# Half splits, unit order, early columns, shorter router chains, float32r put-back and an earlier combine in a two-layer backbone kernel

## The chip, the cores and the metric

The kernel runs on one core of a Trainium2 chip. The metric is the device time of one execution in microseconds (us); before the change the median of 3 runs is 1303.72 us (1302.54 to 1303.9). Engines are named as the profile names them: PE (matmul), PEld (its weight load), DVE (vector), ACT (scalar), POOL (GpSimd), SP (only issues DMAs here).

## What is computed

Two layers over 256 context and 256 latent tokens of width 1024, batch 1. Layer 0 mixes tokens with gated DeltaNet heads and S5 groups, layer 1 with latent attention (MLA); each layer ends with a mixture of 16 experts of which a token takes two. The part that the change touches most, cut from the reference:

```python
def grouped_moe(h, router_w, router_bias, w_gate, w_up, w_down):
    tok = h.reshape(-1, h.shape[-1])
    scores = jax.nn.sigmoid((tok @ router_w).astype(F32))
    choice = scores + router_bias.astype(F32)
    ...  # the best group of 4 experts, in it the best two
    wts = wts / jnp.sum(wts, axis=-1, keepdims=True)
    gates = jnp.sum(jax.nn.one_hot(idx, N_EXPERTS, dtype=F32) * wts[..., None], axis=1)
    for e in range(N_EXPERTS):
        act = jax.nn.silu(tok @ w_gate[e]) * (tok @ w_up[e])
        out = out + gates[:, e:e + 1] * (act @ w_down[e])
...
x = x + g1 * o_l
x = x + g2 * grouped_moe(modulate(x, norm2_g[i], sh2, sc2), ...)   # the context tokens too in layer 0
return rmsnorm(x, final_norm_g)
```

In layer 0 the experts see 512 tokens, in layer 1 the 256 latent ones. An expert's weights are 6 MB in float32, all 32 experts' 201 MB.

## The kernel before

**Stages.** Projections of layer 0 with S5, DeltaNet preparation and the adaLN weights (to about 375 us); DeltaNet solve and scan (to 480); output projection and norm (to 538); router 0 (to 556); experts 0 (to 853); put-back (to 884); MLA (to 1015); output projection 1 and norm (to 1060); router 1 (to 1077); experts 1 (to 1295); final norm.

**Order.** Each engine runs its own queue in order. The last lines of `kernel()` build the program with `schedule_with_timeline_sim=True`: the build lays the order of each queue itself, from the order of the code, the data dependencies and its own estimate of times. So two neighbouring lines need not be neighbours in a queue. `tc.issue_after(ins)` keeps what is written in its block behind `ins` on the same engine. In the first stage five generators are interleaved by hand: each digit of `ORDER` (L42) gives one turn to one of S5, its tables, the chain gates - norm of k - decays - inverses, the projections, and the loads of the adaLN weights (L987).

**Expert weights** come in 1 MB chunks of 128 x 2048 float32, by DMAs on SP's queue, into a ring of slots (9 in layer 0); a chunk is loaded when its slot is free. In layer 0 places 0 and 1 are fixed experts, so their chunks are fetched ahead of the router's result; SP has to read the number of any other expert (`m.exi`) first.

**Experts 0** (L1618 to 1817). Tokens are sorted to tiles of 128 rows, 13 of them, gathered from `h2d`. The units of `order` (L1759) are of three kinds: a *pair* of experts that share a tile, 64 rows each, in float32 (12 MB, 12 chunks); *[1, 2]*, two tiles of one expert; and single tiles of one expert. The last two run in float32r, a quicker matmul type, with both operands split in a hi and a lo part: `wsplit` (L1659) makes hi by an ACT copy and lo = w - hi by DVE or POOL, whole chunks, three hi/lo buffers in turn; `mm3` multiplies xh*wh, xh*wl, xl*wh for each block of 128 rows, so 12 matmuls a chunk. The loop over units runs the gate half 0 of the next unit, turns the activations of this one, runs gate half 1, `write` (down projection, scatter of the rows to `yd` by POOL), then the up halves of the next. For the last unit `put_back` (L1684) is used: its rows are put to the tokens by a one-hot matmul, and `combine` (L1676), called between, reads the two rows of every token from `yd` (four 1 MB reads through the same ring), adds them (POOL), scales and adds them to x (DVE). Then loops over overflow tiles, which run no turn here, make every engine wait for the others.

**Layer 1.** `moe_open` (L1280) loads what the router needs, among it `cols` (L1312): the shift and scale of the second norm as columns, two reads of single elements, 8 KB, from the adaLN result `modd`. PE makes the router's constant `cst` from them, DVE the scaled router weights `rws`, which also need the norm gains `gc2`. It is called inside `out_proj1` (L1252) between the two halves of the projection. `moe_norm` (L1339) makes the logits and, in `late`, h2, on POOL for the last tile of a layer. `experts1` (L1836) takes seven tiles, all in float32, picks the tokens by a one-hot matmul, and `put_back` (L1904) multiplies a gated one-hot `sT` with y in float32: four matmuls a tile. In the trace a float32 matmul leaves two records, a float32r matmul one.

Of the kernel before, what the change touches and what calls it, by code (L numbers as in the profile page):

```python
# [10 lines left out]
F32 = mybir.dt.float32  # L11
F32R = mybir.dt.float32r
I32 = mybir.dt.int32
# [28 lines left out]
ORDER = "14043434201412034140300224440414102414430241041040042342334021201104444404001320040143444401421224440444323042414011111344042423434004400004124041144320420442404440404412324332041440133004030404444034224404143244402404441244"  # L42
# [123 lines left out]
def _build(es, tc, I, O):  # L166
# [75 lines left out]

    n1g = per.tile([128, 2, 8], F32, name="n1g")
    nc.scalar.dma_start(n1g.rearrange("p a b -> p (a b)"), I["norm1_g"])
    mcols = per.tile([128, 2, 2, 2, 8], F32, name="mcols")

# [1040 lines left out]
    def moe_open(l, stack):  # L1287
# [53 lines left out]
    def moe_norm(m, i, t):  # L1341
# [29 lines left out]
    def moe_route(m):  # L1371
# [116 lines left out]
        tt(oh, bc(sm[:, SM_IO16:SM_IO16 + 16, None], SQ), bc(pos[:, None, :], SQ), OP.is_equal)  # L1488
        tt(oh, oh, bc(sm[:, None, SM_IO16:SM_IO16 + 16], SQ), OP.mult)
        red(key[:, :, None], oh, OP.add)  # L1490
        m.exi = rt([128, 16], I32, True)
        V.tensor_copy(m.exi, key)

# [18 lines left out]
        for j in range(2 * n):  # L1512
            kk, i = j // n, j % n
            V.tensor_scalar(m.ohS[:, kk, i], m.io[:, 0:128], rin[:, kk, i], None, op0=OP.is_equal)
# [4 lines left out]
        m.rest = lambda: moe_tables(m, rt, tt, red, oa, sc, table, ovs)  # L1519
# [92 lines left out]
    def experts0(m):  # L1612
        with ExitStack() as st:
# [8 lines left out]
            cnt3, gathers, last_split = [0], [], []  # L1622
# [48 lines left out]
            def mm3(p, xh, xl, wh, wl, start, stop):  # L1671
                mm(p, xh, wh, start, False)
                mm(p, xh, wl, False, False)
                mm(p, xl, wh, False, stop)
# [10 lines left out]
            def put_back(ps_, tok, tok2, gate, between=lambda: None):  # L1685
# [11 lines left out]
                between()  # L1697
# [520 lines left out]
```

## Time and profile before

| | |
|---|---|
| median of 3 runs | 1303.72 us |
| the profiled execution | 1306.65 us, its span 1304.8 us |
| PE busy | 1132.8 us (87%), 6208 matmuls, mean granted clock 0.939 |
| DVE, ACT, POOL busy | 687.2, 420.5, 320.6 us |
| DMA | 342.44 MB, mean 262 GB/s |

The span is the time from the first to the last instruction; the profiled execution's own time is 1.85 us longer. Busy shares are means over stages that have different limits, so they are read by stage. The page's chain of the work that ended last stops at the overflow loop of layer 1, 10 us before the end, and so says nothing of the rest. Granted clock 1.00 is PE at 2.4 GHz, 0.50 at 1.2 GHz.

### The profile page before, as it was taken

What the parts mean: (1) busy time and instruction counts of PE and PEld (TensorE: products, weight loads), DVE (VectorE), ACT (ScalarE), POOL (GpSimd) and SP (SyncE); (2) the same over time, 40 slices, a digit from 0 to 9 for tenths busy, and PEclk for the clock granted to TensorE, in tenths of its full rate; (3) what the DMA queues carried; (4) which work ended last, traced back from release to release, by engine and by line L of the source; (5) the groups of instructions that cost most, each with busy time, mean ns of one, the idle gap of its engine ahead of it and who ended that gap; (6) DMA issues with size and microseconds to landing.
All of it is one profiled execution on the core that took longest, in us unless ns stands there. A gap on an engine that the chain in (4) does not pass through costs nothing. (4 is left out here: it accounts for less than half of the span.)

```text
span 1304.8 us, 17075 instructions
## 1 busy us (share of the span) xinstructions
PE 1132.8 (87%) x6208; PEld 711.9 (55%) x6208; DVE 687.2 (53%) x1393; ACT 420.5 (32%) x694; POOL 320.6 (25%) x249
## 2 busy tenths in 40 slices
PE   4698989998769998598998998867999749999996
PEld 1365656665329987434455646645777645444321
DVE  3979796757954574812325536685576251221122
ACT  3324635452112242112336446615455101100000
POOL 0255553311315330310214213333321020000000
PEclk9799999899879999799998999978999869999998
DMA  8565565688886155879999899453134666999993
GB/s 319 200 206 163 201 204 196 213 295 221 273 218 243 58 184 146 347 268 420 369 381 381 329 397 362 175 229 122 48 132 148 230 274 258 425 425 423 426 425 164
DMA packets 110456, 342.44 MB, mean 262 GB/s; under 512 B 35210, under 2 KB 53002, under 8 KB 84000
## 3 DMA queue, kind: packets, MB, share of 16 engines
q1 hardware_dynamic: 81328, 312.02, 63.0%
q10 hardware_dynamic: 24352, 17.93, 4.5%
q0 software_dynamic: 4688, 11.35, 2.4%
q8 instruction: 51, 0.84, 0.3%
q14 instruction: 37, 0.30, 0.1%
HBM read 319.45 MB, written 26.77 MB: 265 GB/s over the span
## 5 line engine op out<-in xcount | busy, mean ns | idle before, releaser
L209 PE MATMUL ps<-hi,sp 128*128 128x512 f32 x432 | 145.5, 411 | 8.0 <-ACT hi L1667 5.3
L1668 DVE TENSOR_TENSOR lo<-ch,hi 128x2048 fp32r<-128x2048 f32 x40 | 98.5, 2474 | 80.3 <-ACT hi L1667 79.9
L209 PE MATMUL ps<-ch,stat 128*32 128x512 f32 x384 | 91.7, 686 | 28.4 <-DMA ch<-in_ada_w 14.4
L209 PE MATMUL ps<-ch,xT 128*64 128x512 f32 (+1 forms) x488 | 106.8, 596 | 0.0
L209 PEld LDWEIGHTS ps<-hi,sp 128*128 128x128 f32 x432 | 83.4, 195 | 35.1 <-ACT hi L1667 8.5
L1667 ACT ACTIVATE hi<-ch 128x2048 fp32r<-128x2048 f32 x48 | 91.7, 1916 | 29.4 <-issue 10.7
L209 PE MATMUL ps<-lo,sp 128*128 128x512 f32 x216 | 88.9, 412 | 12.8 <-POOL lo L1668 10.0
L209 PE MATMUL ps<-ch,wh 128*64 128x512 f32 x384 | 93.4, 598 | 2.2 <-DMA ch<-in_wu 2.2
L209 PE MATMUL ps<-hH,wh 128*128 128x512 f32 x160 | 66.8, 419 | 5.9 <-ACT hH L658 5.6
L209 PE MATMUL ps<-hH,wl 128*128 128x512 f32 x160 | 65.2, 409 | 1.8 <-DVE wl L605 1.8
L209 PE MATMUL ps<-hL,wh 128*128 128x512 f32 x160 | 66.2, 414 | 0.4 <-DVE hL L659 0.2
L209 PEld LDWEIGHTS ps<-ch,xT 128*64 128x64 f32 (+1 forms) x488 | 32.5, 129 | 58.4 <-issue 57.7
L231 POOL TENSOR_TENSOR frs<-rs,sm 128x1 f32<-128x1 f32 x2 | 1.1, 560 | 234.2 <-DVE rs L230 234.2
L209 PEld LDWEIGHTS ps<-lo,sp 128*128 128x128 f32 x216 | 42.1, 195 | 28.1 <-POOL lo L1668 11.9
L209 PEld LDWEIGHTS ps<-ch,wh 128*64 128x64 f32 x384 | 27.5, 136 | 54.8 <-issue 50.7
L1668 POOL TENSOR_TENSOR lo<-ch,hi 128x2048 fp32r<-128x2048 f32 x8 | 36.6, 4574 | 69.3 <-ACT hi L1667 54.0
L209 PE MATMUL ps<-ch,aT 128*64 128x512 f32 (+1 forms) x232 | 51.9, 596 | 0.7 <-ACTq L1579 0.7
L605 POOL TENSOR_TENSOR wl<-raw,wh 128x1024 fp32r<-128x1024 f32 x16 | 40.8, 2553 | 35.8 <-ACT wh L604 23.3
L1902 DVE TENSOR_TENSOR y<-ps,bcm 128x512 f32<-128x512 f32 x14 | 9.7, 692 | 73.8 <-PE ps L209 73.8
L1627 POOL DMA_INDIRECT xe<-h2d,rt x13 | 15.5, 1193 | 132.3 <-PE ps L206 119.7
L209 PEld LDWEIGHTS ps<-ch,stat 128*32 128x32 f32 x384 | 13.6, 116 | 62.6 <-DMA ch<-in_ada_w 30.4
L209 PE MATMUL ps<-y,sT 128*128 128x512 f32 x72 | 37.9, 659 | 9.5 <-DVE y L1695 7.9
(536 smaller groups left out, 2376.8 us busy)
## 6 DMA issues: line engine op xcount, KB each, us to landing
ch<-in_wg SPq DMA_DIRECT2D x63, 1024.0 KB, 6.4
ch<-in_wu SPq DMA_DIRECT2D x62, 1024.0 KB, 11.1
ch<-in_wd SPq DMA_DIRECT2D x61, 1024.0 KB, 10.6
ch<-in_ada_w SPq DMA_DIRECT2D x88, 512.0 KB, 5.6
raw<-in_w_in SPq DMA_DIRECT2D x16, 512.0 KB, 4.9
bcm<-modd ACTq DMA_DIRECT2D x12, 512.0 KB, 16.2
x<-in_xs SPq DMA_DIRECT2D x8, 512.0 KB, 6.0
yd<-x SPq DMA_DIRECT2D x8, 512.0 KB, 4.9
```

The lines of the kernel that those rows point to most:

```text
L209: return T.matmul(out, l, r, start=start, stop=stop)
L231: G.tensor_tensor(out, t, bc(neghalf, [128, n]), op=OP.pow)
L605: eng.tensor_tensor(wl, w, wh.bitcast(F32), op=OP.subtract)
L1627: g = G.indirect_dma_start(out=xe, out_offset=None, in_=h2d, in_offset=bass.IndirectOffsetOnAxis(ap=idx, axis=0), bounds_check=511, oob_is ...
L1667: last_split[:] = (S.activation(hi, w, AF.Copy), eng.tensor_tensor(lo, w, hi.bitcast(F32), op=OP.subtract))
L1668: eng.tensor_tensor(lo, w, hi.bitcast(F32), op=OP.subtract))
L1902: V.tensor_tensor(j.y[:, nh], p, g2[:, nh * 512:(nh + 1) * 512], op=OP.mult)
```

## The change

- `ORDER` becomes another string of the same 224 digits' counts.
- `wsplit` splits in halves: two ACT copies, then two subtractions, the first on DVE, the second on the engine given; that is POOL for gate half 1 and up half 0 (before: POOL for the whole of up half 0), else DVE. `mm3` becomes `mm3q`: all eight matmuls with hi of a chunk, then the four with lo.
- The units: [1, 2] second, the pairs third, seventh and last, so the last unit is a pair. `combine` stands ahead of the last down projection.
- In `moe_route` the experts' numbers `exi` and `moe_tables` move into `rest`, behind the last one-hot of DVE's queue. In `late` the second multiply goes from POOL to ACT.
- `rope` and `mg` are loaded ahead of router 0, the layer-1 columns (`cols1`) after experts 0.
- In experts 1 `sT` is ungated and float32r, y is scaled by gate and g2 in one DVE operation and split in hi and lo, and the put-back is two float32r matmuls for each one before. The tiles sl, act, aT, sT and y have one buffer.

The diff, cut:

```diff
+    cols1 = per.tile([128, 2, 8], F32, name="cols1")
...
-            cols = m.mh.tile([128, 2, 8], F32, name=f"cols{c}")
-            nc.scalar.dma_start(cols, modd[l, c, 3 * D:5 * D].rearrange("(j k p) -> p j k", j=2, p=128))
+            cols = cols1 if l else m.mh.tile([128, 2, 8], F32, name=f"cols{c}")
+            if l == 0:
+                mod_cols(cols, l, c)
...
-                E.tensor_scalar(h2, h2, m.rstd[:, i:i + 1], None, op0=OP.mult)
+                S.activation(h2, h2, AF.Copy, scale=m.rstd[:, i:i + 1])
...
-        m.rest = lambda: moe_tables(m, rt, tt, red, oa, sc, table, ovs)
+        def rest():
+            with tc.issue_after(last.ins):
+                tt(oh, bc(sm[:, SM_IO16:SM_IO16 + 16, None], SQ), bc(pos[:, None, :], SQ), OP.is_equal)
...
+                V.tensor_copy(m.exi, key)
+                moe_tables(m, rt, tt, red, oa, sc, table, ovs)
...
-                last_split[:] = (S.activation(hi, w, AF.Copy),
-                                 eng.tensor_tensor(lo, w, hi.bitcast(F32), op=OP.subtract))
+                halves = [(slice(0, 2), V), (slice(2, 4), eng)]
+                for s, _ in halves:
+                    S.activation(hi[:, s], w[:, s], AF.Copy)
+                for s, e in halves:
+                    e.tensor_tensor(lo[:, s], w[:, s], hi[:, s].bitcast(F32), op=OP.subtract)
...
+            def mm3q(p, xT, k0, w, start, stop):
+                for q in range(4):
+                    for i in range(2):
+                        mm(p, xT[i][:, k0 + q], w[0][:, q], start and q + i == 0, False)
+                for q in range(4):
+                    mm(p, xT[0][:, k0 + q], w[1][:, q], False, stop and q == 3)
...
-                wh, wl = wsplit(gate_up_chunk(0, name, u[0].es[0](), hh), G if (name, hh) == ("wu", 0) else V)
+                w = wsplit(gate_up_chunk(0, name, u[0].es[0](), hh), G if (name, hh) in (("wg", 1), ("wu", 0)) else V)
...
-            order = [([0], [0, 1]), ([10], [10, 11]), ([1, 2], [2]), ([11], [12, 13]), one[3], one[4], one[5],
-                     ([12], [14, 15]), one[6], one[7], one[8], one[9]]
+            order = [([0], [0, 1]), ([1, 2], [2]), ([10], [10, 11]), one[3], one[4], one[5],
+                     ([11], [12, 13]), one[6], one[7], one[8], one[9], ([12], [14, 15])]
...
+            combine()
             p = [p for _, _, p in down(cur)]
-            put_back(p, m.tokf[:, cs], tokm[:, cs], m.gate[:, cs], combine)
+            put_back(p, m.tokf[:, cs], tokm[:, cs], m.gate[:, cs])
...
-                V.tensor_scalar(j.sT, m.io, j.tok, j.gate, op0=OP.is_equal, op1=OP.mult)
+                V.tensor_scalar(j.sT, m.io, j.tok, None, op0=OP.is_equal)
...
-                    V.tensor_tensor(j.y[:, nh], p, g2[:, nh * 512:(nh + 1) * 512], op=OP.mult)
+                    V.scalar_tensor_tensor(y, p, j.gate, g2[:, nh * 512:(nh + 1) * 512], op0=OP.mult, op1=OP.mult)
+                    parts_of(hi, lo, y, V)
...
-                        mm(p, j.sT[:, i * 128:(i + 1) * 128], j.y[:, nh], True, True)
+                        for part, y in enumerate(j.y):
+                            mm(p, j.sT[:, i * 128:(i + 1) * 128], y[:, nh], part == 0, part == 1)
...
+    nc.scalar.dma_start(rope.rearrange("p a b c -> p (a b c)"), I["c_rope"])
+    nc.scalar.dma_start(mg, I["mla_g"])
...
+    mod_cols(cols1, 1, 0)
```

## Rows read from the trace of the kernel before

**Rows 1.** Stages: window, length; PE, PEld, DVE, ACT, POOL busy; clock, DMA share, GB/s.

```profile
538.00:556.00 18.00, 3.01 (x62) 2.56 (x62) 16.36 (x83) 0.26 (x1) 5.91 (x3) 0.50 0.96 403
556.00:853.00 297.00, 273.36 (x1200) 163.51 (x1197) 122.67 (x87) 133.86 (x124) 73.52 (x33) 0.97 0.85 339
853.00:884.20 31.20, 18.51 (x46) 10.01 (x44) 26.28 (x23) 0.60 (x1) 11.25 (x4) 0.78 0.59 229
...
1077.00:1282.00 205.00, 202.53 (x1040) 84.13 (x1042) 36.81 (x70) 18.01 (x29) 0.00 (x0) 0.99 0.96 399
```

**Rows 2.** Waits of PE, 556 to 885: total us, times, longest us.

```profile
PE ps L209 <- POOL lo L1668: 10.0, 4, 3.4
...
PE ps L209 <- ACT hi L1667: 5.3, 4, 1.6
...
PE ps L209 <- DVE lo L1668: 2.7, 4, 1.3
PE ps L209 <- DMA ch<-in_wu: 2.2, 1, 2.2
```

**Rows 3.** In order of time, experts 0: start, us, engine, operation [idle before].

```profile
611.33 2.28 DVE L1668 TENSOR_TENSOR lo<-ch,hi 128x2048 fp32r<-128x2048 f32 x1
628.47 4.54 POOL L1668 TENSOR_TENSOR lo<-ch,hi 128x2048 fp32r<-128x2048 f32 x1
629.66 5.52 DVE L1668 TENSOR_TENSOR lo<-ch,hi 128x2048 fp32r<-128x2048 f32 x1 [16.04 <-ACT hi L1667]
692.12 0.79 PE L209 MATMUL ps<-lo,sp 128*128 128x512 f32 x1 [3.42 <-POOL lo L1668]
```

**Rows 4.** Groups of instructions, whole span: busy us, mean ns of one.

```profile
L1667 ACT ACTIVATE hi<-ch 128x2048 fp32r<-128x2048 f32 x48 | 91.7, 1916 | 29.4 <-issue 10.7
...
L605 POOL TENSOR_TENSOR wl<-raw,wh 128x1024 fp32r<-128x1024 f32 x16 | 40.8, 2553 | 35.8 <-ACT wh L604 23.3
...
L604 ACT ACTIVATE wh<-raw 128x1024 fp32r<-128x1024 f32 x16 | 16.9, 1056 | 35.1 <-PE ps L209 19.1 <-DMA dcd<-x 6.6 <-DMA raw<-in_w_in 5.6
```

**Rows 5.** In order of time: PE at the same place of two single units.

```profile
800.61 0.49 PE L209 MATMUL ps<-hi,sp 128*128 128x512 f32 x1 [1.13 <-ACT hi L1667]
...
820.85 0.50 PE L209 MATMUL ps<-hi,sp 128*128 128x512 f32 x1 [1.13 <-ACT hi L1667]
821.82 0.50 PE L209 MATMUL ps<-hi,sp 128*128 128x512 f32 x1 [0.47 <-ACT sp L1640]
```

**Rows 6.** In order of time: the end of layer 0.

```profile
853.61 2.20 SPq L1680 DMA_DIRECT2D ch<-yd  x4
858.68 11.34 POOL L1681 TENSOR_TENSOR ch<-ch 128x1024 f32<-128x1024 f32 x4 [7.35 <-DMA ch<-yd]
872.35 10.11 PE L209 MATMUL ps<-y,sT 128*128 128x512 f32 x16 [7.90 <-DVE y L1695]
881.67 2.47 DVE L1702 TENSOR_TENSOR x<-x,ps 128x512 f32<-128x512 f32 x4
```

**Rows 7.** In order of time: the output projection of layer 1.

```profile
1039.83 1.22 DVE L1305 SCALAR_TENSOR_TENSOR bcm<-bcm,bcm 128x1024 f32<-128x1024 f32 x1 [4.78 <-DMA bcm<-modd]
1041.94 3.56 PE L209 MATMUL ps<-rw,cols 128*128 128x16 f32 x16 [7.67 <-DMA cols<-modd]
1045.34 7.02 PE L209 MATMUL ps<-ch,oT 128*128 128x512 f32 x22
1054.65 0.69 DVE L1214 TENSOR_TENSOR opt<-ps,bcm 128x512 f32<-128x512 f32 x1 [0.33 <-PE ps L209]
```

**Rows 8.** Two windows, columns as in Rows 1.

```profile
1035.00:1050.00 15.00, 8.06 (x29) 7.15 (x30) 4.19 (x7) 0.00 (x0) 0.57 (x1) 0.54 0.35 113
...
1280.00:1285.00 5.00, 4.24 (x21) 1.71 (x22) 0.00 (x0) 0.60 (x1) 0.00 (x0) 1.00 0.45 185
```

**Rows 9.** In order of time: PE at the end of experts 1.

```profile
1287.78 3.65 PE L209 MATMUL ps<-ch,aT 128*64 128x512 f32 x14
1292.21 1.98 PE L209 MATMUL ps<-y,sT 128*128 128x512 f32 x4 [0.79 <-DVE y L1902]
```

**Rows 10.** Waits of PE, 90 to 480, as in Rows 2.

```profile
PE ps L209 <- DMA ch<-in_ada_w: 11.0, 8, 3.5
```

More of the change, by code (lines that the diff above doesn't have):

```diff
@@ L241, in _build @@
     V.memset(adab, 0.0)
+    rope = per.tile([128, 2, 2, 32], F32, name="rope")
+    mg = per.tile([128, 5], F32, name="mg")
     n1g = per.tile([128, 2, 8], F32, name="n1g")
@@ L1513, in moe_route @@
             kk, i = j // n, j % n
-            V.tensor_scalar(m.ohS[:, kk, i], m.io[:, 0:128], rin[:, kk, i], None, op0=OP.is_equal)
+            last = V.tensor_scalar(m.ohS[:, kk, i], m.io[:, 0:128], rin[:, kk, i], None, op0=OP.is_equal)
         if l == 0:
@@ L1621, in experts0 @@
             V.tensor_scalar(tokm, m.tokf, -256.0, None, op0=OP.add)
-            cnt3, gathers, last_split = [0], [], []
+            cnt3, gathers = [0], []
             def gather(idx):
@@ L1740, in down @@
                         continue
-                    wh, wl = wsplit(down_chunk(0, u[0].es[0](), nh), V)
+                    w = wsplit(down_chunk(0, u[0].es[0](), nh), V)
                     for j in u:
                         p = ps(2)
-                        for q in range(4):
-                            mm3(p, j.aT[0][:, q], j.aT[1][:, q], wh[:, q], wl[:, q], q == 0, q == 3)
+                        mm3q(p, j.aT, 0, w, True, True)
                         yield nh, j, p
@@ L1778, in experts0 @@
             unit(0)
-            unit(1)
+            job(order[1][0][0], order[1][1])
             fetch(2)
@@ L1843, in pick @@
                 for i in range(2):
[L1844 removed]
+                    s = w2.tile([128, 128], F32, tag=f"sl{i}", bufs=1, name=nm("sl"))
                     V.tensor_scalar(s, m.ohS[:, 0, i], hot(0, i), None, op0=OP.mult)
@@ L1879, in gated @@
             def gated(j):
-                j.a = w2.tile([128, 512], F32, tag="act", name=nm("act"))
+                j.a = w2.tile([128, 512], F32, tag="act", bufs=1, name=nm("act"))
                 S.activation(j.a, j.wg, AF.Silu)
@@ L1884, in turned @@
             def turned(j):
-                j.aT = w2.tile([128, 4, 128], F32, tag="aT", name=nm("aT"))
+                j.aT = w2.tile([128, 4, 128], F32, tag="aT", bufs=1, name=nm("aT"))
                 p = ps(3)
@@ L1891, in down @@
             def down(j):
-                j.sT = w2.tile([128, 256], F32, tag="sT", name=nm("sT"))
-                V.tensor_scalar(j.sT, m.io, j.tok, j.gate, op0=OP.is_equal, op1=OP.mult)
-                j.y = w2.tile([128, 2, 512], F32, tag="y", bufs=1, name=nm("y"))
+                j.sT = w2.tile([128, 256], F32R, tag="sT", bufs=1, name=nm("sT"))
+                V.tensor_scalar(j.sT, m.io, j.tok, None, op0=OP.is_equal)
+                j.y = [w2.tile([128, 2, 512], F32R, tag=f"y{i}", bufs=1, name=nm("y")) for i in "hl"]
                 for nh in range(2):
@@ L1901, in down @@
                             mm(p[c, :], j.aT[:, q, c], wch[b][:, q, :], q == 0, q == 3)
-                    V.tensor_tensor(j.y[:, nh], p, g2[:, nh * 512:(nh + 1) * 512], op=OP.mult)
+                    hi, lo = (y[:, nh] for y in j.y)
+                    y = w2.tile([128, 512], F32, tag="y", bufs=1, name=nm("y"))
+                    V.scalar_tensor_tensor(y, p, j.gate, g2[:, nh * 512:(nh + 1) * 512], op0=OP.mult, op1=OP.mult)
+                    parts_of(hi, lo, y, V)
             def put_back(j):
@@ L2003, in _build @@
     krH, krL = (l1.tile([128, 512], F32R, name=n) for n in ("krH", "krL"))
-    rope = l1.tile([128, 2, 2, 32], F32, name="rope")
-    nc.scalar.dma_start(rope.rearrange("p a b c -> p (a b c)"), I["c_rope"])
-    mg = l1.tile([128, 5], F32, name="mg")
-    nc.scalar.dma_start(mg, I["mla_g"])
+    mod_cols(cols1, 1, 0)
     def apply_rope(pool, dst, src, t, nh):
```

26 lines of the change are left out of this document (9 added, 17 removed).

## The prediction

> **What bounds the kernel now.** I read the windows by stage first, then PE's waits, then the order of time in the three places where PE stands still. The reader should see that no one engine bounds the whole: the matmul engine carries the layer-0 experts and stands still in the two routers, and DMA carries the layer-1 experts.
>
> Four stages matter [rows 1]. In the layer-0 experts (556 to 853) PE is busy 273.4 of 297 us, and DVE and ACT less than half of it, so PE's own work is the floor, and the gain to be had is the 24 us in which it waits. From 853 to 884.2 the layer's results are read back and added: DVE is busy 26.3 of 31.2 us, PE 18.5. The router (538 to 556) is a chain of 83 DVE operations, PE busy 3.0 of 18. In the layer-1 experts (1077 to 1282) the DMA share is 0.96 at 399 GB/s while PE is busy 202.5 of 205: both are full, so PE work taken out there shortens nothing until the weights have landed.
>
> The profiled execution took 1306.65 us, 1.85 more than its span of 1304.8, and 2.93 more than the median of the runs. The sum is made against 1306.65 and then carried to the median.
>
> **Part 1, layer-0 experts: half splits, matmul order, unit order.** Each chunk of a single expert is split into hi (ACT) and lo (DVE, or POOL for one chunk in six). Before, the second matmul of a chunk already needs lo, and POOL takes 4.54 us for it, so PE waits: 3.42 us in the case shown, 10.0 in four cases; ACT's hi costs 5.3, DVE's lo 2.7, and 2.2 went to a weight DMA [rows 2, 3]. That is 20.2 of the stage's 24 us.
>
> After, hi comes in two halves, lo in two halves on one or two engines, and eight hi matmuls run before the first lo. A half costs ACT 1.06 us and POOL 2.55 [rows 4]; DVE's is half of 2.28, 1.15 [rows 3]. A single unit repeats every 20.24 us with 1.6 us of waits in it [rows 5], so its 84 matmuls and transposes take 0.22 each. From the first hi half on PE has ten matmuls (2.2 us) before it needs POOL's half, which is there 1.06 + 2.55 = 3.6 us later: the 3.42 wait becomes 1.4, and 10.0 becomes about 4.1. DVE's half (1.15) is there before eight matmuls (1.8) are through: 2.7 becomes 0. ACT's first half is ready 1.92 - 1.06 = 0.86 us sooner in each of four waits [rows 4]: 5.3 becomes 1.9. The DMA wait came because two pairs stood first, and a pair asks for 12 MB where the double unit asks for 6; with the double unit second I put it at 0. Left: 6.0 of 20.2, a gain of 14. The number of matmuls is the same. The extra ACT time (12 halves of 1.06 for 6 of 1.92, 1.2 us a unit) lies beside PE, as ACT is busy 133.9 of 297 [rows 1]; without that cover it would cost 8 x 1.2 = 10 us. PE's slower pace after a long wait (0.79 for the first lo matmul after the 3.42, 0.50 after a shorter wait [rows 3, 5]) is left to the range. Bounds: 0 to -20.
>
> Against this speaks a row: while POOL's lo ran (628.47 to 633.01) a DVE lo took 5.52 us instead of 2.28, which is POOL's remaining 3.3 us plus its own time [rows 3]. The new form puts a POOL half and a DVE half on one chunk. The Trainium skill ("SBUF — State Buffer", section "SBUF: two separate sides") says that the two engines share one port pair as an exclusive lock held for the whole instruction; this trace agrees. By that rule the halves of one chunk queue up rather than overlap; it is the slower rival below.
>
> **Part 2, combine ahead of the last put-back.** Before, the yd reads are issued at 853.61, POOL adds for 11.34 us, the put-back matmuls wait 7.90, start at 872.35 and take 10.11 for 8, and the last x add ends at 884.14 [rows 6]; the granted clock of the stage is 0.78 [rows 1]. After, a pair is last, with no splits; the reads are placed before the down projection, and the adds can run beside it. But they wait for the scatter of the unit before, they are 4 MB ahead of or between the four 1 MB down chunks on SP, and those chunks get three of their slots only when the pair's up chunks have been consumed. At 399 GB/s [rows 1] a MB takes 2.6 us. If all four reads go first, down waits about 10 us and the adds save about as much: 0, or 3 worse. If down's chunks go first, the reads end under the down matmuls, and some 9 us go. Behind the waiting read on SP stand down's chunks and then the layer-1 input weights, which nobody needs before 884. I take -3, nearer the bad end, as the code asks for the reads first.
>
> **Part 3, early columns.** In the layer-1 output projection PE waits 7.67 us, to 1041.94, for the columns, the last DMA on ACT's queue, behind two 512 KB rows, of which the second released DVE at 1039.83. Then 16 constant matmuls take 3.56 us and 22 of the projection 7.02, and the last projection sum is there at 1054.65 [rows 7]. With the columns loaded a stage earlier PE goes on at 1034.27. From 1035 to 1050 the mean granted clock was 0.54, near the lower level, 1.2 GHz [rows 8]; at full clock the two groups take about 1.8 and 22 x 0.22 = 4.9 us. That is 7.67 + 1.8 + 2.1 = 11.6 less. The scaled router weights still wait for the norm gains, issued just ahead of the columns on the same queue; with DVE's 1.22 and two small operations they can be there at about 1041.5, and PE reaches them at 1034.27 + 1.8 + 4.9 = 1041.0. So nothing else is much late; I take -11. Bounds: -4 (PE is queued on those weights before the projection) and -12. The moved load itself is one 8 KB DMA on ACT's queue where the rope load was; rope and mg go one stage up, no one waits for them: 0. The layer-1 weights are fetched ahead into the same slots and stop when these are full, so the earlier start is passed on.
>
> **Part 4, layer-1 put-back in float32r.** Two float32 put-back matmuls take 1.98 us [rows 9], the four of a tile 4; eight float32r matmuls of 0.22 take 1.8. Seven tiles: some 15 us of PE, but DMA is full, so it counts only at the end. There DMA's share is 0.45 in the 5 us from 1280 [rows 8], so the last weights land near 1282.3, while PE starts on them at 1287.78 and ends at 1291.43 [rows 9]: it is 5.5 us behind. Freed of the put-backs it stands ready: 1282.3 + 3.65 = 1286. The last put-back's chain grows by an ACT hi and a DVE lo of 512 columns (about 0.53 and 0.57, by the halves of part 1), and its matmuls are 1 us shorter: +0.5 with the handing over. So -5. Behind PE's new wait for lo stands the next tile's up projection, for which PE has slack. The single buffers for act, aT, sl, sT and y cost nothing, as their readers run a chunk earlier on PE; if one stalls, the same slack covers it. Bounds 0 and -7.
>
> **Part 5, shorter router chains.** 17 of the 83 DVE operations leave each chain, 0.2 us each by the mean [rows 1], 3.3 us at most, partly in gaps; they return behind the last one-hot. In layer 0 the gathers come sooner, but the tables' last matmul, behind which the third of the adaLN weights is queued, comes later: -1.5, bounds -3.3 and +2. The experts' numbers come later too; SP needs one for its ninth chunk, and eight static ones are ahead of it (DMA share 0.96 there): 0. In layer 1 the first pick is queued behind the same operations: 0, bounds -3.3 and +2.5. The h2 multiply on ACT takes work off POOL where nobody waits: 0.
>
> **Part 6, the order string.** Each generator has as many turns as before, in another order. The trace of before can't price that. The nearest row is PE's wait for the adaLN weights there, 11.0 us in eight cases [rows 10]; most of them could go, and as much could come. I take 0, bounds -8 and +8.
>
> **Sum.** -14 - 3 - 11 - 5 - 1.5 + 0 = -34.5: 1306.65 - 34.5 = 1272.15, and less 2.93 the median is 1269.
>
> **Rivals.** *Another wait takes the columns' place*: PE's queue has the router matmuls ahead of the projection. It then stands until 1041.5 and does the projection at half clock, ending at 1050.5 instead of 1054.6; 4 gained, not 11: 1276. For it: the rows on ACT's queue are unchanged. Against: before, 22 projection matmuls stood ahead of them. *The splits don't pay* (chunk halves are queued so that PE's order or ACT's stays the limit): part 1 brings 2, not 14: 1281. For it: within a single unit PE's waits are for hi and for the activations' split, not for lo [rows 5]. *Slower, the port lock*: each of the eight split units has two POOL halves against two DVE halves; uncovered, each meeting costs 2.55 + 1.15 = 3.7 us, 7.4 a unit. The other parts give 20.5, so it decides from 2.6 us a unit on above 20.24; with half of it uncovered it is 8 x 3.7 = 30 us and no gain: 1269 + 14 + 30 = 1313. Against: lo on DVE and POOL fills 5 x 2.28 + 4.54 = 15.9 us of a unit now and 10 x 1.15 + 2 x 2.55 = 16.6 after. *Better*: order string and combine at their good ends: 1255.
>
> **How the numbers follow.** Forecast 0.48 (1260 to 1278), columns' rival 0.18 (1276), splits don't pay 0.20 (1281, to 1290 with a bad order string), better 0.07, port lock 0.07. The range for 8 in 10 leaves out most of the last two: 1251 to 1292. A measurement of this kernel can tell about 0.2% from no change; faster by more 0.92, within it 0.02, slower 0.06.
>
> **What would show it.** PE's wait for columns gone and the last projection sum 11 us sooner after the attention; PE's waits for lo in layer 0 near 4 us, for hi near 2; a single unit near 19.3 us; the last weights and PE's last down matmuls within 4 us of each other. Wrong if the stage before 375 us changes by more than 8 us, if a DVE half lo often takes over 3 us, or if down's chunks land behind the yd reads.

## The result and the profile after

The changed kernel takes 1294.03 us at the median of 4 runs (1291.24 to 1295.86), against 1303.74 for the kernel before in the same rounds: 0.9926 of its time (0.9904 to 0.9947). The forecast was 1269 (1251 to 1292). The direction is right and the gain, 9.7 us, is less than a third of the 34.5 that the sum gave; the time lies 2 us outside the range. The profiled execution took 1295.31 us, its span 1293.5; against the span of before that is 11.3 us.

The stages that answer to [rows 1] and [rows 7], by the windows of the kernel after: window, length; PE, PEld, DVE, ACT, POOL busy; clock, DMA share, GB/s. Each window goes from an event to an event (last logits of layer 0; first expert matmul; end of the last activation transposes; last x add; then issue of the second norm's gains to last logits of layer 1; first weight matmul of experts 1 to the start of their last activation transposes).

```profile
544.25:576.27 32.02, 10.14 (x102) 4.80 (x101) 21.36 (x92) 3.78 (x5) 6.09 (x5) 0.61 0.66 259
576.27:840.94 264.67, 259.28 (x1149) 160.47 (x1148) 136.10 (x121) 133.57 (x169) 68.66 (x38) 1.00 0.93 370
840.94:876.31 35.37, 17.45 (x48) 5.62 (x48) 23.59 (x20) 0.60 (x1) 12.11 (x4) 0.76 0.62 248
...
1014.87:1044.51 29.64, 23.80 (x123) 20.73 (x122) 10.96 (x19) 4.62 (x7) 4.16 (x4) 0.86 1.00 409
1067.71:1267.83 200.12, 190.68 (x1001) 80.23 (x1001) 44.81 (x85) 24.03 (x39) 0.00 (x0) 1.00 0.99 407
```

The same events in the kernel before, and the differences (us; with the output projection of layer 0, -0.3, which is left out, the rows add up to the span's -11.3 but for rounding):

| from event to event | before | after | difference |
|---|---|---|---|
| start to the scan's last sums | 476.44 | 482.38 | +5.9 |
| last logits of layer 0 to token table | 17.13 | 17.47 | +0.3 |
| token table to first expert matmul | 7.84 | 14.55 | +6.7 |
| first expert matmul to last x add | 320.59 | 300.04 | -20.6 |
| MLA | 139.87 | 138.56 | -1.3 |
| norm gains' issue to last logits of layer 1 | 36.01 | 29.64 | -6.4 |
| last logits of layer 1 to first weight matmul | 22.00 | 23.20 | +1.2 |
| first weight matmul to last activation transposes | 197.99 | 200.12 | +2.1 |
| from there to the end | 24.79 | 25.67 | +0.9 |

So the experts gave more than the 17 that parts 1 and 2 were to give. Three stretches that the sum had at nought or below took back 15: the start to the scan's last sums, the gap between router and experts, and layer 1's experts.

The waits of PE from 530 to 900, to be held against [rows 2] (total us, times, longest):

```profile
PE ps L209 <- SPq L1591: 16.8, 2, 16.4
...
PE ps L206 <- ACT wh L1662: 4.4, 1, 4.4
...
PE ps L209 <- DVE lo L1683: 1.5, 2, 0.8
...
PE ps L209 <- POOL lo L1683: 1.0, 3, 0.3
```

PE's wait for lo fell from 12.7 us to 2.5. But a wait of 16.4 us on SP's queue is new, and so is one of 4.4 us for `wh`, the copy of the first tile's transposed rows.

### The profile page after: what moved, and what is told of

It reads as the page before. It is cut to its first block, busy times and chain, and to the rows that moved or that the text cites. A ratio compares the mean times of both kernels' runs of the same rounds, so it can differ in the third digit from the quotient of the medians.

```text
span 1293.5 us, 17219 instructions
## 1 busy us (share of the span) xinstructions
PE 1118.3 (86%) x6208; PEld 711.3 (55%) x6208; DVE 705.4 (55%) x1447; ACT 432.0 (33%) x757; POOL 316.0 (24%) x255
## 5 line engine op out<-in xcount | busy, mean ns | idle before, releaser
L1683 DVE TENSOR_TENSOR lo<-ch,hi 128x1024 fp32r<-128x1024 f32 x80 | 112.0, 1442 | 57.6 <-ACT hi L1681 57.4
L209 PE MATMUL ps<-hi,sp 128*128 128x512 f32 x432 | 112.4, 400 | 1.3 <-ACT y L1766 1.3
L209 PE MATMUL ps<-ch,wh 128*64 128x512 f32 x384 | 97.7, 613 | 17.2 <-SPq L1591 16.8
L1681 ACT ACTIVATE hi<-ch 128x1024 fp32r<-128x1024 f32 x96 | 94.2, 1056 | 35.8 <-DMA ch<-in_wg 27.8
L209 PEld LDWEIGHTS ps<-hi,sp 128*128 128x128 f32 x432 | 79.4, 188 | 27.1 <-issue 5.7
L209 PE MATMUL ps<-lo,sp 128*128 128x512 f32 x216 | 63.7, 403 | 2.5 <-DVE lo L1683 1.5
L1683 POOL TENSOR_TENSOR lo<-ch,hi 128x1024 fp32r<-128x1024 f32 x16 | 42.1, 2629 | 86.9 <-ACT hi L1681 53.9
L1918 DVE SCALAR_TENSOR_TENSOR y<-ps,rt,bcm 128x512 f32<-128x512 f32 x14 | 10.5, 751 | 63.5 <-PE ps L209 63.5
L1150 POOL TENSOR_TENSOR ch<-ch,ch 128x512 fp32r<-128x512 f32 (+1 forms) x28 | 31.5, 1155 | 53.8 <-PE ps L209 29.9
L749 DVE SCALAR_TENSOR_TENSOR ac<-ps,convw,ac 128x510 f32<-128x510 f32 (+1 forms) x48 | 35.5, 739 | 12.7 <-ACT ac L745 12.4
```

The source lines that it names most:

```text
L209: return T.matmul(out, l, r, start=start, stop=stop)
L749: V.scalar_tensor_tensor(ac[:, :, lo:hi], pv[:, :, lo + o:hi + o], convw[:, blk, j:j + 1], ac[:, :, lo:hi], op0=OP.mult, op1=OP.add)
L1150: eng.tensor_tensor(lo, src, hi.bitcast(F32), op=OP.subtract)
L1681: S.activation(hi[:, s], w[:, s], AF.Copy)
L1683: e.tensor_tensor(lo[:, s], w[:, s], hi[:, s].bitcast(F32), op=OP.subtract)
L1918: V.scalar_tensor_tensor(y, p, j.gate, g2[:, nh * 512:(nh + 1) * 512], op0=OP.mult, op1=OP.mult)
```

## Experiments

Each ratio is against the kernel before in the same rounds. The changed kernel was not run again beside its variants, and the medians of the kernel before move from 1302.4 to 1306.4 us from set to set. So lengths of stages, from one profiled execution each, carry more of the argument than differences of medians.

**Where the router's gap comes from.** The expert numbers (`m.exi`) are computed behind the last one-hot after the change. One run puts these five operations back where they were.

```diff
+        tt(oh, bc(sm[:, SM_IO16:SM_IO16 + 16, None], SQ), ...)   # ahead of the one-hots again
...
+        V.tensor_copy(m.exi, key)
...
             with tc.issue_after(last.ins):
-                ...  # the same five operations
                 moe_tables(m, rt, tt, red, oa, sc, table, ovs)
```

> The changed kernel with one part undone: the five operations that make the experts' numbers stand in the router's chain again, not behind its last one-hot. Theory A (the late number costs): the queue of the loads stands still from 547 to 564 us for the number of the ninth chunk, the chunk lands at about 572.7, and the copies of the first tile's transposes stand behind its hi split on ACT. With the number some 7 us sooner the chunk lands before the transposes are done, ACT's wait goes, and the first expert matmul comes 3 to 5 us sooner (576.3 to about 572), even though the five operations put about 1 us back into the chain: 1294 becomes 1289 to 1291. Theory B (the chunk is late because the loads in flight keep DMA full): the first expert matmul stays within 1 us of 576, the chain is 1 us longer: 1294 to 1295.

Measured: 1289.12 us, 0.9853 (0.9805 to 0.9901) of before. Router 0 in order of time (start, us, engine, operation, idle before); first after, then with the numbers early:

```profile
562.66 0.17 DVE L1529 CAST rt<-rt 128x16 int32<-128x16 f32 x1
...
564.12 0.36 SPq L202 DMA_DIRECT2D ch<-in_wg  x1
...
572.73 2.00 ACT L1681 ACTIVATE hi<-ch 128x1024 fp32r<-128x1024 f32 x2 [27.19 <-DMA ch<-in_wg]
...
574.63 0.58 ACT L1662 ACTIVATE wh<-ps 128x512 f32<-128x512 f32 x1
...
575.27 1.07 PE L206 MATMUL ps<-cm,xe 128*128 128x128 f32 x4 [4.38 <-ACT wh L1662]
```

```profile
555.08 0.17 DVE L1500 CAST rt<-rt 128x16 int32<-128x16 f32 x1
556.53 19.45 SPq L202 DMA_DIRECT2D ch<-in_wg  x2
...
568.34 2.01 ACT L1681 ACTIVATE hi<-ch 128x1024 fp32r<-128x1024 f32 x2 [22.84 <-PE ps L209]
...
571.38 0.66 PE L206 MATMUL ps<-cm,xe 128*128 128x128 f32 x4 [0.81 <-ACT wh L1662]
```

After the change the number is there at 562.66, SP issues the ninth chunk at 564.12, 1.5 us behind it, and ACT's hi halves of that chunk wait for the landing until 572.73. The first tile's copy `wh` is queued behind them on ACT, and PE's transposes behind the copy. Before the change SP stood still for the number in the same way (there 548.31, the issue at 549.69); it was only there sooner. With the number early all this ends 4 us sooner, and the time from the token table to the first expert matmul falls from 14.55 to 9.81 us. The five operations put 0.5 us back into the chain, so from the last logits to the first expert matmul 32.02 us become 27.76: 4.3 of the 7.0 lost.

**What the rest of the gap is.** The best kernel, below, with its tables held behind the last one-hot and the numbers in the chain:

```diff
+            last = V.tensor_scalar(m.ohS[:, kk, i], ...)
...
+            with tc.issue_after(last.ins):
                 moe_tables(m, rt, tt, red, oa, sc, table, ovs)
```

> The kernel of s9 with the router tables held behind the last one-hot, as in the change, but with the experts' numbers left in the chain and h2 left on POOL. It asks whether the shorter chain pays once the late number and the multiply on ACT are out. In s9 the token table stands 17.1 us behind the last logits and the first expert matmul 7.7 us behind that; in e1 these were 18.0 and 9.8. Theory A (the prediction: 12 operations of 0.2 us leave the chain and come back where nobody waits): 15 to 16 and 7.7, 1 to 2 us faster in layer 0. Theory B (what leaves the chain in front of the token table comes back in front of the adaLN matmuls, behind which the first transposes are queued): 15.5 to 16.5 and 9.5 to 10, together 0 to 1 us longer. The whole is then 1274 within a microsecond and a half either way, so the two stretches decide.

Measured: 1280.35 us, 0.9815 (0.9785 to 0.9846). From the last logits of layer 0 to the first expert matmul it takes 27.42 us, against 24.86 without the edit, and in layer 1 from the last logits to the first pick matmul 19.03 against some 17.5. In its order of time:

```profile
550.74 5.76 PE L209 MATMUL ps<-ch,stat 128*32 128x512 f32 x32
...
558.48 1.94 PE L209 MATMUL ps<-ch,wh 128*64 128x512 f32 x8
```

The adaLN matmuls (the first row) stand behind the tables' last matmul and ahead of the experts; they start 19.7 us behind the last logits, without the edit 17.6. The prediction named this queue, and took it for smaller than the gain. The two together cost 2.5 us: the token table, which the shorter chain was to bring sooner, comes 17.05 us behind the last logits instead of 17.14.

**Whether the reads block the last down projection.** One run asks for the last pair's four down chunks ahead of the yd reads.

```diff
+            wds = [[down_chunk(0, e(), nh) for e in cur[0].es] for nh in range(2)]
             combine()
...
+                pair(p[nh], cur[0].aT, 0, wds[nh], 4)
```

> The changed kernel with the four down chunks of the last pair asked for ahead of the four yd reads; the adds still stand ahead of the put-back. Theory A (the reads in front of the chunks on the load queue cause PE's wait): PE's wait of 16.4 us ahead of the last down projection falls under 3 us, the down matmuls run from about 842 to 853, the adds beside them, and the last x add ends 6 to 10 us sooner (876.3 to 866 to 870): 1294 becomes 1284 to 1288. Theory B (the POOL adds and the two DVE operations of each token tile bound the end, 4 x 2.4 and 4 x 2.5 us, in whatever order the loads stand): PE's wait goes, but the last x add stays within 2 us of 876: 1292 to 1295.

Measured: 1291.05 us, 0.9884 (0.9843 to 0.9924). The end of layer 0 in order of time, after and then with the chunks first:

```profile
841.98 2.37 SPq L1698 DMA_DIRECT2D ch<-yd  x4
...
844.55 2.15 SPq L202 DMA_DIRECT2D ch<-in_wd  x4
...
847.19 2.33 POOL L1699 TENSOR_TENSOR ch<-ch 128x1024 f32<-128x1024 f32 x1 [12.73 <-DMA ch<-yd]
...
857.32 1.94 PE L209 MATMUL ps<-ch,wh 128*64 128x512 f32 x2 [16.39 <-SPq L1591]
...
875.62 0.69 DVE L1719 TENSOR_TENSOR x<-x,ps 128x512 f32<-128x512 f32 x1 [0.17 <-PE ps L209]
```

```profile
843.37 8.78 PE L209 MATMUL ps<-ch,wh 128*64 128x512 f32 x32 [1.26 <-ACT y L1766]
...
848.79 2.21 SPq L1698 DMA_DIRECT2D ch<-yd  x4
...
853.94 12.36 POOL L1699 TENSOR_TENSOR ch<-ch 128x1024 f32<-128x1024 f32 x4 [8.79 <-DVE y L1713]
...
874.42 1.28 DVE L1719 TENSOR_TENSOR x<-x,ps 128x512 f32<-128x512 f32 x2
```

PE's wait of 16.4 us is gone, its down matmuls start 14 us sooner, and the last x add ends at 875.7 instead of 876.3. The reads went 6.8 us later by the same edit, and POOL's adds with them. After the change PE comes last, as each of the last x adds waits 0.17 us for it; with the chunks first the adds of POOL and DVE come last, and the last x adds wait for nothing. Whichever goes first, the other sets the end, and the two ends lie 0.6 us apart: the wait had been the largest of PE's, and taking it away gained nearly nothing.

**Which part gives the experts' gain.** The kernel before with the half splits, their matmul order and POOL's places alone, none of the rest; and the kernel before again.

```diff
-                last_split[:] = (S.activation(hi, w, AF.Copy), ...)
+                halves = [(slice(0, 2), V), (slice(2, 4), eng)]
...
-                wh, wl = wsplit(..., G if (name, hh) == ("wu", 0) else V)
+                w = wsplit(..., G if (name, hh) in (("wg", 1), ("wu", 0)) else V)
...
+                    mm3q(getattr(j, name), j.xT, 4 * hh, w, hh == 0, hh == 1)
```

> The kernel before with the half splits and the new matmul order in layer 0's experts alone (old unit order, old combine, all else as before). From the first expert matmul to the last x add of layer 0 the kernel before takes 320.6 us, the changed one 300.0. Theory A (the prediction's part 1: 14 us, of which 2.2 go with the unit order): 308.5, the whole 12 us faster, 0.991 of before. Theory B (half splits bring all of the gain, unit order and early combine nothing): 300 to 302, 0.985 of before. Theory C (half of the gain is the unit order's): about 310, 0.992.

> The kernel before, unchanged, profiled on the chip of this set. Theory A (the later inverses, 392.4 to 394.4 us in the five profiles of the changed kernel and its variants against 389.8, and the slower weights' DMA in layer 1, 419 to 420 GB/s against 424 to 425, belong to the changed kernels): here the wait for the decays ends at 389 to 390.5 and the rate is 424 to 425. Theory B (both differ from execution to execution or from chip to chip): the wait ends at 391 to 394, the rate is 419 to 421.

Measured: 1283.58 us, 0.9835 (0.9785 to 0.9885); the kernel before, a single execution, 1307.18. This part alone is quicker than the whole change. Its windows (first expert matmul to last activation transposes, then to the last x add) and its waits of PE from 556 to 829:

```profile
559.28:827.39 268.11, 261.31 (x1157) 159.09 (x1156) 134.87 (x119) 134.65 (x169) 69.28 (x37) 1.00 0.91 369
827.39:860.04 32.65, 17.13 (x40) 9.54 (x40) 24.99 (x24) 1.76 (x3) 13.73 (x5) 0.69 0.56 227
```

```profile
PE ps L209 <- DVE lo L1671: 1.6, 3, 0.9
...
PE ps L209 <- ACT hi L1669: 0.6, 1, 0.6
...
PE ps L209 <- POOL lo L1671: 0.4, 1, 0.4
```

From the first expert matmul to the last x add it takes 300.8 us, 19.8 less than before; with unit order and early combine it takes 300.0. So these two bring 0.8 at most, and that is not clear of the spread: over all profiled executions with the halves it takes 299.3 to 303.5 us without the two (6) and 298.6 to 302.8 with them (7). From the start of the last activation transposes to the last x add it takes 33.3 us without them, against 28.4 before: the experts end sooner, and the scatter, reads and adds behind them do not follow in full (the reads are issued 6.5 us behind that start, before 2.1 us ahead of it). From the first expert matmul on, PE's granted clock went from 0.98 (563.55 to 855.70 before; [rows 1] begins 7.55 us earlier) to 1.00, and its waits for hi and lo from 18.0 us [rows 2] to 2.6.

**The columns alone, and the gains with them.** The kernel before with layer 1's columns loaded behind experts 0; and the kernel after with early numbers, the old order string and the norm gains loaded beside the columns.

```diff
+    cols1 = per.tile([128, 2, 8], F32, name="cols1")
...
+            cols = cols1 if l else m.mh.tile([128, 2, 8], F32, name=f"cols{c}")
...
+    mod_cols(cols1, 1, 0)
+    nc.scalar.dma_start(gain1, I["norm2_c"][:, 8:16])   # the second run only
```

> The kernel before with the columns of layer 1 loaded behind experts 0, all else as before (the rope table and mg where they were). From the issue of the norm gains to the last logits the kernel before takes 36.0 us, the changed one 29.6. Theory A (the prediction: 11 us, nothing else is late): 25, 0.9915 of before. Theory B (the scaled router weights, which still wait for the gains behind two 512 KB rows, are late by 2 to 3 us, and DVE's queue by as much again): 29 to 30, 0.995 of before. Theory C (the change of 29.6 came from other parts): 33 or more, 0.998.

> The changed kernel with the experts' numbers back in the router's chain, the order string of before, and the norm gains of layer 1 (4 KB) loaded with the columns, ahead of MLA. The first two are known from their runs: 4.3 and 2 to 3 us. Theory A (the gains are what the scaled router weights wait for): PE's wait of 2.6 us for them goes, and the last logits come 2.5 to 5 us sooner after the attention (29.6 to 25 to 27 us): 1283 to 1285. Theory B (DVE's queue, the 1.2 us operation on the row and the 2.5 us of h2 in front of the copies of h2T, sets the logits): under 1 us, 1286 to 1288.

Measured: 1300.66 (0.9975, 0.995 to 1.0) and 1284.22 us (0.9843, 0.9796 to 0.989). The columns alone are hardly told from no change by the whole time, whose interval reaches 1; the stage shows them. With them the stage from the gains' issue to the last logits takes 29.8 us instead of 36.0, as in the kernel after, whose output projection of layer 1 reads in order of time:

```profile
1024.88 5.83 PE L209 MATMUL ps<-ch,oT 128*128 128x512 f32 x24
...
1033.57 0.17 DVE L1321 SCALAR_TENSOR_TENSOR cols<-cols,gc 128x8 f32<-128x8 f32 x1 [1.21 <-DMA gc<-in_norm_c]
...
1034.21 1.04 PE L209 MATMUL ps<-rws,h2T 128*128 128x16 f32 x8 [2.63 <-DVE rws L1323]
...
1038.35 1.89 PE L209 MATMUL ps<-rws,h2T 128*128 128x16 f32 x8 [3.11 <-DVE h2T L1359]
```

PE's 7.67 us for the columns [rows 7] are gone; next it stands 2.63 us for the scaled weights, which wait for the gains, and 3.11 us for copies of h2T in DVE's queue. With the gains early the first of these goes: from the last x add of layer 0 to the last logits of layer 1 it is 164.6 us, against 168.2 after and 175.9 before (167.0 and 166.4 in the best kernel below, which loads both early too). The wait for h2T stays.

**The parts that pay, together.** The halves with columns and gains loaded early, nothing else of the change; the two share a tile of 512 bytes a partition. It was run twice, on two chips.

```diff
+    spare = per.tile([128, 128], F32, name="spare")
+    cols1, gain1 = spare[:, 0:16].rearrange("p (j k) -> p j k", j=2), spare[:, 16:24]
...
+    with tc.issue_after(mod_cols(cols1, 1, 0).ins):
+        nc.scalar.dma_start(gain1, I["norm2_c"][:, 8:16])
```

> The kernel before with three things: the half splits with their matmul order, and the columns and norm gains of layer 1 loaded behind experts 0, these two in one tile of 512 bytes a partition (columns alone were 64). Unit order, combine, order string, router chains, put-back and rope table as before. Expected from the earlier runs: half splits 320.6 to 300.8 us (first expert matmul to last x add), last logits 168 to 165 us after that add (176 in the kernel before), so 1272 to 1276, faster than both kernels. It also tests a cause of the slower weights' DMA (420 GB/s in every kernel whose permanent pool grew by 64, 96 or 596 bytes a partition, 424 to 425 in those where it did not grow). Theory A (the addresses of the ring slots: what counts is a shift that is no multiple of 512 bytes): 424 to 425 GB/s here. Theory B (any shift, or the early loads themselves): 419 to 421.

> The kernel of s9 once more, beside the next one on the same chip: 1272 to 1277. It also shows whether its gain over the kernel before (0.977) comes back in other executions.

Measured: 1274.35 us, 0.9769 (0.9733 to 0.9804), and again 1277.50, 0.9804 (0.977 to 0.9839). It beats both kernels.

**Put-back and order string.** The kernel after with the old float32 put-back and its buffers; with the old string; the halves with the new string; the best kernel with the new string.

```diff
-                j.sT = w2.tile([128, 256], F32R, tag="sT", bufs=1, name=nm("sT"))
+                j.sT = w2.tile([128, 256], F32, tag="sT", name=nm("sT"))
...
-                        for part, y in enumerate(j.y):
-                            mm(p, j.sT[:, i * 128:(i + 1) * 128], y[:, nh], part == 0, part == 1)
+                        mm(p, j.sT[:, i * 128:(i + 1) * 128], j.y[:, nh], True, True)
```

> The changed kernel with layer 1's put-back of before: gated one-hot, float32, four matmuls a tile, two buffers each. Theory A (the prediction: PE is freed of 15 us and stands ready at the end): without it PE ends 4 to 5 us later after the last weights, 1294 becomes 1298 to 1299. Theory B (the time between the last weights and the last down matmuls, 5.5 us before and 6.4 us after, is the chain of the last unit itself, up matmuls, activation, transposes, first down half; the put-backs of the tiles ahead were hidden behind the weights' DMA): the last down half starts 5 to 7 us behind the last weights in this kernel too, and the end is 0 to 1.5 us sooner by the shorter chain of the last put-back: 1292.5 to 1294.

Measured: 1291.70 us, 0.9887 (0.9847 to 0.9928). The end of experts 1, after and then with the old put-back (a window as above, then order of time):

```profile
1268.00:1270.00 2.00, 1.25 (x8) 0.59 (x9) 0.00 (x0) 0.60 (x1) 0.00 (x0) 1.00 0.53 213
```

```profile
1275.85 3.65 PE L209 MATMUL ps<-ch,aT 128*64 128x512 f32 x14
...
1281.00 1.46 PE L209 MATMUL ps<-y,sT 128*128 128x512 f32 x4 [1.51 <-ACTq L1591]
```

```profile
1266.00:1268.00 2.00, 1.25 (x8) 0.48 (x8) 0.00 (x0) 0.60 (x1) 0.00 (x0) 1.00 0.51 209
```

```profile
1273.29 3.65 PE L209 MATMUL ps<-ch,aT 128*64 128x512 f32 x14
...
1277.71 1.99 PE L209 MATMUL ps<-y,sT 128*128 128x512 f32 x4 [0.78 <-DVE y L1916]
```

A DMA share near 0.5 in a window of 2 us puts the end of the weights' stream at its middle: 1269.0 and 1267.0 (an estimate). PE's last run of down matmuls starts 6.8 and 6.3 us later, with the new put-back no sooner than with the old. A few packets land behind the stream, the last at 1271.4, 1268.8 and, in the kernel before, 1283.3; from them it is 4.4, 4.5 and 4.4 us, so nothing changed. What PE does ahead of it, after the change:

```profile
1258.58 1.46 PE L209 MATMUL ps<-y,sT 128*128 128x512 f32 x4 [0.84 <-ACT y L1149]
1259.97 3.22 PE L209 MATMUL ps<-ch,xT 128*64 128x512 f32 x13
1262.60 0.59 PE L209 MATMUL ps<-x,xT 128*64 128x512 f32 x1
...
1267.83 0.66 PE L206 MATMUL ps<-cm,act 128*128 128x128 f32 x4 [0.78 <-DVE act L1896]
1269.23 4.50 PE L209 MATMUL ps<-ch,aT 128*64 128x512 f32 x18 [0.75 <-ACT aT L1903]
```

Four down chunks of 1 MB come behind the last up chunk; at 420 GB/s each takes 2.5 us, so that up chunk was there at about 1269.0 - 10.0 = 1259.0 (an estimate). PE starts on the pair of chunks to which it belongs only at 1262.60, 3.6 us later: up to 1259.97 it puts back the unit before, and then it has the first up half to finish. That put-back takes from 1257.01 to 1259.97, 2.96 us, as PE waits for hi and lo of y; in float32 it took 3.03 (1254.62 to 1257.59 with the old put-back).

> The changed kernel with the order string of before. Theory A (the string is what made the first stage longer): the wait for the decays ends at about 389.8 instead of 392.8, router 0 starts at about 538.6 instead of 544.2, and all of it reaches the end: 1294 becomes 1288 to 1289. Theory B (only the 3 us up to the inverses come from the string, the 2.7 us in the scan from elsewhere): 1291. Theory C (the two strings do equally well and the two profiles differ by chance): 1294.

> The kernel before with the half splits and the new order string, nothing else. The half splits alone took 1283.6 us, with the wait for the decays over at 385.1 and the scan's last sums at 472.3; the changed kernel and its variants with the new string have 391.6 to 394.4 and 481.5 to 483.2. Theory A (the string costs the first stage and the start of the solve 4 to 9 us): 388 or more and 477 to 483, 1288 to 1292. Theory B (only the scan's 2 us are the string's, the rest belongs to the rope table's load, which the build has put at the start of ACT's queue, or to chance): 385 to 389 and 474 to 478, 1284 to 1287.

> The kernel of s9 with the new order string, nothing else. Theory A (the string costs as much as s10 against r6 showed): 4 to 5 us more than the kernel of s9 on the same chip, PE's waits for the adaLN weights in the first stage at 18 to 21 us against 12 to 18, and the scan's last sums 4 to 9 us later. Theory B (only the scan's start is the string's): 1 to 2 us more. Theory C (no difference): within 1 us.

Measured: 1291.81 us (0.9879, 0.9833 to 0.9925), 1288.18 (0.987, 0.9823 to 0.9916) and 1279.16 (0.9812, 0.9778 to 0.9846). The new string is 2.2, 4.6 and 1.7 us slower in the three pairs, each pair with overlapping times, and only the last pair on one chip: it does not help, and a cost of that size is not clear of the spread. PE's waits from 90 to 480, the best kernel again with the old string and then with the new:

```profile
PE ps L209 <- DMA ch<-in_ada_w: 17.0, 8, 4.3
```

```profile
PE ps L209 <- DMA ch<-in_ada_w: 16.5, 13, 4.3
```

The wait for the adaLN weights by which the prediction bounded the string is as long with the old one. The wait for `XC`, a tile of the first stage, is 3.8 us with the new and 1.1 with the old, but in the kernel before it was 4.1 with the old, so it does not tell the strings apart either.

**The rope table's place.** The change loads `rope` and `mg` ahead of the layer-0 experts in the code; nothing holds them there, and in the trace after they stand at 19.3 us, early on ACT's queue. One run puts them back, and the columns in a tile of 512 bytes.

```diff
-    rope = per.tile([128, 2, 2, 32], F32, name="rope")
...
+    rope = l1.tile([128, 2, 2, 32], F32, name="rope")
```

> The changed kernel with the rope table and mg loaded where they were before, and the columns in a tile of 512 bytes a partition instead of 64 (so the permanent pool grows by 512 bytes instead of 596). Theory A (slot addresses and the early rope load cost): weights' DMA in layer 1 at 424 to 425 GB/s, 2 us less from the first layer-1 weight matmul to the end, and the scan's last sums 2 to 5 us sooner than 482: 1287 to 1290. Theory B (neither counts): 420 GB/s, 481 to 483, 1294. If only the rate returns: 1291 to 1292.

Measured: 1292.85 us over 8 runs, 0.9905 (0.9876 to 0.9934), 1.2 less than after. Its profiled execution, the quickest of the eight, reached the scan's last sums at 473.7 us instead of 482.4. Over all profiled executions this event comes so (mean, count and span of the times):

| | old string | new string |
|---|---|---|
| rope, mg where they were | 474.0 (7; 470.3 to 476.9) | 477.0 (3; 473.7 to 478.9) |
| rope, mg ahead | 480.2 (2; 479.8 to 480.6) | 482.5 (4; 481.5 to 483.2) |

Kernels with the loads ahead are all later than those without. Yet the median of the run that puts them back says 1 us, not 9, and those with the loads ahead also have their slots elsewhere. What makes the first stage longer stays open.

## Why the prediction was wrong in size

**Halves, order and combine (-14 and -3).** The mechanism was right, and the halves are under-sized: 19.8 alone, where 14 was forecast. PE's waits for hi and lo fell to 2.6 us, where 6.0 were to stay; and the slower pace after a wait, left to the range, went too (granted clock 0.98 to 1.00, PE busy 266 to 261 us up to the last transposes). The part's -3 for the combine is 0.8 at most, with unit order. The prediction had two cases, by which DMAs go first, and gave 9 us to the one with down's chunks first; both ended alike, because with the reads first PE's down projection ends last, and with the chunks first the reads, POOL's adds and the adds to x do.

**The port lock** did not decide. The halves by group of instructions, after (busy us, mean ns, idle before):

```profile
L1683 DVE TENSOR_TENSOR lo<-ch,hi 128x1024 fp32r<-128x1024 f32 x80 | 112.0, 1442 | 57.6 <-ACT hi L1681 57.4
...
L1683 POOL TENSOR_TENSOR lo<-ch,hi 128x1024 fp32r<-128x1024 f32 x16 | 42.1, 2629 | 86.9 <-ACT hi L1681 53.9
```

A DVE half takes 1.44 us on average, where 1.15 was estimated: most take 1.22, but 7 of the 80 over 3. So the two engines do meet, the sign that the prediction named against itself, but PE's waits for lo are 2.5 us in all: the eight hi matmuls in front leave little of it to be seen. The lock shows where nothing covers it, in router 0:

```profile
545.47 2.34 POOL L1374 TENSOR_TENSOR h<-h,bcm 128x1024 f32<-128x1024 f32 x1 [1.26 <-ACT h L1373]
545.57 2.29 DVE L1401 TENSOR_SCALAR rt<-rt 128x64 f32<-128x64 f32 x1 [1.09 <-ACT rt L1399]
```

DVE's first operation of the chain, on 64 columns, lasts as long as POOL's add beside it, 2.29 us; operations of that size take some 0.2. The Trainium skill ("SBUF — State Buffer", section "SBUF: two separate sides") describes an exclusive lock held for the whole instruction; the trace agrees, as DVE ends 0.05 us behind POOL. The kernel before had the same meeting at another operation of the chain, of 128x16, which took 1.60 us beside POOL's add, so the change made it some 0.7 us worse.

**Router chains (-1.5).** The step that failed is "SP needs one for its ninth chunk, and eight static ones are ahead of it ...: 0". SP reads the number in order, so all its later loads wait for it, and the ninth chunk is now of a split unit, whose hi copies stand on ACT ahead of the first tile's. It cost 4.3 us of 7.0; the tables' last matmul with the adaLN work behind it, bounded at +2, cost about 2.5. The 1.5 us themselves did not come either: from the last logits to the token table it takes 17.47 us with 68 DVE operations, where it took 17.13 with 82.

**Columns (-11).** The mechanism was right, and the size lies between the forecast (11) and the rival (4): 6.4. The rival's reason was wrong: after the change the projection stands ahead of the scaled weights on PE (24 of its matmuls in the 5.83 us from 1024.88, above) and waits for nothing there. The step that failed is "nothing else is much late": 2.63 us for the gains and 3.11 for DVE's copies of h2T were, 5.7 of the 11 together.

**Put-back (-5).** The failing step is "Freed of the put-backs it stands ready". The 5.5 us between the last weight and PE's start on it did not go with the quicker put-back: it is 6.8 us, with the old one 6.3. Two things fill them. PE comes to the last up chunks 3.6 us late, behind the put-back of the unit before, and there the new form saves 0.1 us, since its matmuls wait for hi and lo. Behind that stands the last unit's own chain: up matmuls to 1267.05, activation and transposes to 1269.23, the first down half and its put-back, 13.25 us from 1262.60 to 1275.85 without another unit's work between, where the four down chunks need 10.0; 3.6 + 13.25 - 10.0 gives the 6.8. The tail grew by 0.8 us, where +0.5 was forecast: PE waits 1.51 us for ACT's hi instead of 0.78 for DVE's product.

**Order string (0, -8 to +8)** and first stage: +5.9 at the scan's last sums, inside the bounds. By the means above the string accounts for some 2 to 3 of it and the place of the loads for some 6, neither of them shown. With the same code up to there the event came between 470.3 and 476.9, so one pair of executions cannot share it out.

In sum, the 23.2 us between the forecast of the sum and the result (34.5 less 11.3) are the router of layer 0 with 8.6 (-1.5 to +7.0), put-back and layer 1's experts with 8.0 (-5 to +3.0), the stages up to the router with 5.7, the columns with 4.6 and the router of layer 1 with 1.2; the layer-0 experts, 3.6 better, and MLA, 1.3, run the other way.

## What to carry to other kernels

A value that an in-order load queue reads is on the path of every load behind it, even when many loads stand ahead: move its computation later only if the next loads are not needed soon. Before a gap between the last weight and the last matmul is read as backlog, subtract the last unit's own chain, and price a quicker form of the work in front with its new waits, not by its matmuls alone. And of a bundle of edits, time the parts alone: here one part and a half (1274 to 1278 us) is worth nearly three times the whole (1294).

## What the runs showed of the hardware

Layer 1's weights came at two rates, which go with the place of their slots. The windows from 1150 to 1200 of the kernel after, the columns alone, the best kernel, and the one with rope put back (last column GB/s):

```profile
1150.00:1200.00 50.00, 50.00 (x300) 20.44 (x302) 14.73 (x28) 6.59 (x11) 0.00 (x0) 1.00 1.01 420
```

```profile
1150.00:1200.00 50.00, 50.00 (x280) 22.13 (x280) 10.63 (x19) 4.78 (x8) 0.00 (x0) 1.00 1.01 420
```

```profile
1150.00:1200.00 50.00, 50.00 (x293) 20.27 (x289) 8.92 (x14) 3.89 (x7) 0.00 (x0) 1.00 1.01 425
```

```profile
1150.00:1200.00 50.00, 50.00 (x298) 20.53 (x295) 13.22 (x24) 6.10 (x10) 0.00 (x0) 1.00 1.01 424
```

The slots lie behind the kernel's permanent tiles. Where these are as before or 512 bytes a partition larger, it is 423 to 425 GB/s (9 profiled executions of 7 kernels); where they are 64, 596 or 628 larger, 419 to 421 (7 kernels). Both rates stand side by side on one chip, and the early loads themselves don't make the difference: the best kernel has them and 425. But no run moved the slots and nothing else. (The expectation of the best kernel's first run gives 96 for what is 628.) Over 200 us a hundredth is 2 us, the size of the stage's +2.1, though the stage's length itself (197.8 to 199.0 and 198.6 to 201.5) overlaps. The Trainium skill's "DMA: Bandwidth & Descriptors", section "How a descriptor splits into AXI transactions", says that a transaction starts at a multiple of 256 bytes and that a descriptor which does not costs more beats; it speaks of what is fetched. The measurement agrees in direction, for the side that is written; a shift of 256 itself was not run, and the cause stays open.
